# One more column for the row sum: weighted sums of an attention block in 64-column products, copied out by ScalarE

## The chip, the cores and the metric

The kernel runs on one core of a Trainium2 chip. TensorE (PE) multiplies matrices and writes PSUM, VectorE (DVE), ScalarE (ACT) and GpSimd (POOL) work on vectors, and SyncE (SP) issues the DMAs. The metric is the device time in microseconds of one execution. Three runs of the kernel before took 625.96, 629.58 and 630.68 us, a median of 629.58 us.

## The reference

One layer over 1024 real frames with 16 meta tokens in front. After an RMS norm and one input projection there are 16 attention heads of 64 value columns: 8 "fox" heads (causal, with a decay that is added to the logits) and 8 "MLA" heads (masked by chunks of 64 frames, keys and queries from low-rank latents). Each head's result is gated, and all go through one output projection, a norm and a residual. What the change touches is the softmax and its weighted sum:

```
s = einsum('bqhd,bkhd->bhqk', q[:, q0:q0 + Q_BLOCK], k[:, :kend]) * scale
s = mask_and_bias(s, q0, kend)
p = softmax(s, axis=-1)
out = einsum('bhqk,bkhd->bqhd', p, v[:, :kend])
```

The softmax is the exponential of each logit less its row's maximum, over the sum of the row.

## The kernel before, in words

The kernel has three stages. Up to about 172 us it normalizes and transposes x, and projects the latents and the values. From 172 to about 590 us it runs the 16 heads, and beside them the projections of the next heads, the gates and, late, half of the output projection. The last 39 us are the rest of the output projection and the final norm.

All large products are made in float16 with a high and a low part of each operand, as hi·hi + hi·lo + lo·hi. So the values lie in `Vt` as two blocks of 64 columns for each block of keys and head, the high part and the low part.

A head runs in four steps (`STEPS`, L701), each with two blocks of 128 rows: (7,0), (6,1), (5,2), (4,3). `run_head` calls `step` (L891) for each, so there are 64 steps. One call of `step` does, for the new pair n: the scores on PE (L800, the mask L803); the peaks of the rows on DVE (`peaks`, L810 to L815, of which `nbs` in L815 is the bias for the exponentials); the exponentials on ACT (L823). Each exponential reads the scores out of PSUM, writes `pr`, and adds up its row in `sums` by `accum_out`, which is a second instruction, ACTIVATION_READ_ACCUMULATOR. Then ACT casts the high part of the pair to float16 (`high`, L836). For the pair before, DVE makes the low part (`low`, L840) and SP issues the DMA that transposes both parts into `pT` (L919). For the pair three steps back (`LAG`) PE makes the weighted sums (`weighted`, L842), and DVE adds their two halves into `onat` (L931). The scores' PSUM buffers are free for the next pairs when the exponentials have read them: there are two of the large kind (`s2`) and one of the small kind (`s1`, blocks 0 to 2 and the end of block 7). There is one buffer `avs` for the weighted sums.

In `weighted` each block j of transposed probabilities is a stationary operand. Its high part meets the high and the low values at once, 128 columns (L849), and its low part meets the high values, 64 columns (L848). One step has 11 products of the first kind and 9 of the second, and every product has its own weight load. After a head's last step `head_end` takes the reciprocals of the row sums and GpSimd scales the head's result (L857); in the last head `tiles_end` does this for each step on DVE.

The order of the instructions on each engine is not written out: a scheduler of the framework orders each engine's queue by its own estimate of when things are ready. Each engine works its queue in order.

Of the kernel before, what the change touches and what calls it, by code (L numbers as in the profile page):

```python
# [28 lines left out]
H = 8  # L29
# [19 lines left out]
def hybrid_kernel(ctx, tc, x, meta, norm_pre, norm_post, w_in, b_f, q_norm, w_uq, kv_norm, w_ukv, w_out,  # L49
# [380 lines left out]
    def latents_V(t):  # L430
        lh, ll = lts.pop(t)
        pv = psa("pv")
        T.matmul(pv, lh, wv_h.rearrange("p h d -> p (h d)"), start=True, stop=False)
        T.matmul(pv, lh, wv_l.rearrange("p h d -> p (h d)"), start=False, stop=False)
        T.matmul(pv, ll, wv_h.rearrange("p h d -> p (h d)"), start=False, stop=True)
        vm = xs.tile([P, H, 2, HD], F16, name="vm", tag="vm", bufs=1)
        split_v(pv, scale_mu, vm[:, :, 0, :], vm[:, :, 1, :])
        SY.dma_start(vm_d[:, :, t].rearrange("h p k d -> p h k d"), vm)

    def values_out(t, ps):  # L440
        split_v(ps, scale_fu, Vt[:, t, 1 : H + 1, 0, :], Vt[:, t, 1 : H + 1, 1, :])

    def values(t):
        ps = psa("ps2")
# [373 lines left out]
    def exponentials(i, parts, nb, inv, pr, sums):  # L818

        c0 = 0  # L820
        for part, c in zip(parts, (i, NT)):
# [20 lines left out]
    def weighted(av, i, hi, lo, vh):  # L842

        n = i + 1
        avf = av.rearrange("p t d -> p (t d)")
        for j in range(n + 1):
            if j > 0:
                T.matmul(avf[:, 0:HD], lo[:, j - 1, :], Vt[:, j, vh, 0], start=False, stop=False)  # L848
            T.matmul(avf, hi[:, j, :], Vt[:, j, vh].rearrange("p t d -> p (t d)"), start=j == 0, stop=j == n)  # L849

    def head_end(onat, hh, sums):

        V.tensor_tensor(sums[:, NT - 1 : NT], sums[:, NT - 1 : NT], sums[:, NT : NT + 1], ALU.add)
        rs = at.tile([P, NT], F32, name="rs", tag="rs", bufs=2)
        V.reciprocal(rs, sums[:, 0:NT])
        o = onat[:, :, hh * HD : (hh + 1) * HD]
        G.tensor_tensor(o, o, rs.unsqueeze(2).to_broadcast([P, NT, HD]), ALU.mult)  # L857

    extras = {}
    gates = {}  # L860
# [26 lines left out]
            fn()  # L887

    steps = {}

    def step(first):  # L891

        now[0] += 1
        n = now[0]
        if first is not None:
            (ia, ib), passes, mask, mask_w, inv, sums = first[0:6]
# [11 lines left out]
            steps[n] = dict(t=(ia, ib), pr=prs, prw=pr, ph=ph, phs=(ph, ph[:, B0 * P :]), los=los, rest=first[6:])  # L908
        evacuate()
        prev = steps.get(n - 1)  # L910
        if prev is not None:
            for i, p, h, l in zip(prev["t"], prev["pr"], prev["phs"], prev["los"]):
                low(i, p, h, l)
            ph, n1 = prev["ph"].rearrange("p (b k) -> p b k", k=P), prev["prw"].rearrange("p (b k) -> p b k", k=NM)
            w0 = 1 + 8 * (prev["t"][0] + 1)
            G.tensor_tensor(ph[:, 0 : B0 + 1 : B0, 96:112], n1[:, 0 : w0 + 1 : w0, :],  # L916
                            ph[:, 0 : B0 + 1 : B0, 112:128], ALU.subtract)
            prev["pT"] = at.tile([P, NBLK * P], F16, name="pT", tag="pT", bufs=3).rearrange("p (b k) -> p b k", k=P)
            SY.dma_start_transpose(prev["pT"], prev["ph"])  # L919
        if first is not None:  # L920
            for i, p, h in zip((ia, ib), prs, steps[n]["phs"]):
                high(i, p, h)
        for fn in agenda.pop(n, ()):
            fn()
        old = steps.pop(n - LAG, None)
        if old is not None:
            (ia, ib), pT = old["t"], old["pT"]
            vh, onat, hh, after = old["rest"]
            weighted(avs[:, 1], ia, pT, pT[:, B0 + ib + 2 :, :], vh)
            weighted(avs[:, 0], ib, pT[:, B0:, :], pT[:, ia + 2 :, :], vh)  # L930
            V.tensor_reduce(onat[:, ib : ia + 1 : ia - ib, hh * HD : (hh + 1) * HD], avs.rearrange("p i t d -> p i d t"),  # L931
                            AX.X, ALU.add)
            if after is not None:
                after(ia, ib)

    def run_head(head, vh, hh, passes, mask, mask_w, inv, onat, after, each=None):

        sums = at.tile([P, NT + 1], F32, name="sums", tag="sums", bufs=2)

        def end(ia, ib):  # L940
            head_end(onat, hh, sums)
            if after is not None:
                after()

        ends = [None] * (len(STEPS) - 1) + [end]
        if each is not None:
            ends = [lambda ia, ib: each(ia, ib, sums)] * len(STEPS)

        total = sum(j[1] for j in jobs if j[0] == head)
        for k, tiles in enumerate(STEPS):  # L950
            step((tiles, passes, mask, mask_w, inv, sums, vh, onat, hh, ends[k]))
# [282 lines left out]

    def load_values(h):

        SY.dma_start(Vt[:, :, h], vm_d[h])

    later(3, lambda: load_values(0))
    for h in range(H - 1):  # L1240
# [87 lines left out]


    chains = deque()  # L1330
    ended = []

    def tiles_end(ia, ib, sums):
        if ia == NT - 1:
            V.tensor_tensor(sums[:, ia : ia + 1], sums[:, ia : ia + 1], sums[:, NT : NT + 1], ALU.add)
        both = slice(ib, ia + 1, ia - ib)
        rs = at.tile([P, 2], F32, name="rs2", tag="rs2", bufs=2)
        V.reciprocal(rs, sums[:, both])
        o = onat[:, both, HD:P]
        V.tensor_tensor(o, o, rs.unsqueeze(2).to_broadcast([P, 2, HD]), ALU.mult)  # L1340
        ended.append(sums)

        def chain():
            ps = ps_1.tile([P, 512], F32, name="pso", tag="s1")
            og = at.tile([P, 512], F32, name="og", tag="og", bufs=2)
            for k, t in enumerate((ib, ia)):
                c = slice(k * P, (k + 1) * P)
                T.transpose(ps[:, c], onat[:, t, :], ident)
                V.scalar_tensor_tensor(og[:, c], ps[:, c], OUTK, gates[7, t // 4][:, t % 4 * P : (t % 4 + 1) * P],
                                       ALU.mult, ALU.mult)  # L1350
            hi, lo = (og_part(7, k).rearrange("p (t k) -> p t k", k=P)[:, both, :] for k in range(2))
            split(og[:, 0 : 2 * P].rearrange("p (t k) -> p t k", k=P), hi, lo, A, V)
        chains.append(chain)
    for h in range(H):
# [15 lines left out]
        if h == H - 1:  # L1370
# [7 lines left out]
            for z in range(2):  # L1378
                for k in range(2):
# [9 lines left out]
    gpost = fin.tile([P, D], F32, name="gpost")  # L1389
    SY.dma_start(gpost, norm_post[0:1, :].to_broadcast([P, D]))  # L1390
    rows = {}
    slots = deque([(None, "row", 1), (at, "onat", 2)] + [(at, "pr", 2)] * 2 + [(at, f"ph{k}", 1) for k in range(NPH)]
                  + [(at, "pT", 3)] * 3 + [(at, "onat", 2), (None, "row", 1)] + [(at, "pr", 2)] * 2 + [(at, f"ph{k}", 1) for k in range(NPH)])

    def row(name):
        pl, tag, bufs = slots.popleft()
        if pl is None:
            return fin.tile([P, D], F32, name=name, tag="row", bufs=1)
        w = {"onat": D, "pr": 2 * NM + 9 * P}.get(tag, NBLK * P // 2)
        return pl.tile([P, w], F32, name=name, tag=tag, bufs=bufs)[:, 0:D]  # L1400

    def load_rows(t):
# [115 lines left out]
```

## Time and profile before

| | |
|---|---|
| median of three runs | 629.58 us (625.96 to 630.68) |
| the profiled execution | 630.68 us, of which span 628.9 us |
| PE busy, DVE busy, ACT busy | 556.4 (88%), 484.3 (77%), 422.7 (67%) |
| attention, 172 to 590 us: PE, DVE, ACT | 380.1, 336.1, 293.0 of 418 us |
| granted TensorE clock, mean | 0.979 |

The profiled execution is the slowest of the three. The span runs from the first to the last instruction; the rest of its 630.68 us lies around it. A busy PE includes the tail of each product, so its matmuls overlap in the rows; what one product costs in a stream is the distance between two starts.

### The profile page before, as it was taken

What the parts mean: (1) busy time and instruction counts of PE and PEld (TensorE: products, weight loads), DVE (VectorE), ACT (ScalarE), POOL (GpSimd) and SP (SyncE); (2) the same over time, 40 slices, a digit from 0 to 9 for tenths busy, and PEclk for the clock granted to TensorE, in tenths of its full rate; (3) what the DMA queues carried; (4) which work ended last, traced back from release to release, by engine and by line L of the source; (5) the groups of instructions that cost most, each with busy time, mean ns of one, the idle gap of its engine ahead of it and who ended that gap; (6) DMA issues with size and microseconds to landing.
All of it is one profiled execution on the core that took longest, in us unless ns stands there. A gap on an engine that the chain in (4) does not pass through costs nothing.

```text
span 628.9 us, 11509 instructions
## 1 busy us (share of the span) xinstructions
PE 556.4 (88%) x4130; PEld 330.5 (53%) x4130; DVE 484.3 (77%) x1001; ACT 422.7 (67%) x852; POOL 194.6 (31%) x282
## 2 busy tenths in 40 slices
PE   2999799989798998999998986978879979988994
PEld 1445454546456565666665553655545555554542
DVE  3778876566778886878885768789988887778666
ACT  5688877546778776657677556677785785768222
POOL 2223333362324243323331322223222322320343
PEclk9999999989899999999999998999999999999998
DMA  8858777175666988696957696597986795796963
GB/s 298 207 132 224 148 197 190 33 202 140 127 175 128 206 196 137 117 210 134 175 106 175 129 210 144 111 178 132 174 181 127 129 205 119 158 223 129 299 239 133
DMA packets 269528, 105.02 MB, mean 167 GB/s; under 512 B 234832, under 2 KB 257360, under 8 KB 269472
## 3 DMA queue, kind: packets, MB, share of 16 engines
q1 hardware_dynamic: 269472, 104.30, 73.5%
q8 instruction: 32, 0.52, 0.3%
q14 instruction: 24, 0.20, 0.1%
HBM read 48.38 MB, written 13.96 MB: 99 GB/s over the span
## 4 chain that ended last, share of the span: by engine, by line
PE 30%; DVE 26%; ACT 22%; issue 9%; DMA 9%; SPq 2%; POOL 1%; ACTq 0%; DVEq 0%; POOLq 0%
ACT pr L823 9%; DVE ph L840 5%; DVE nb L810 5%; ACT ph L836 4%; DMA pT<-ph 3%; PE psg L973 3%; PE psg L974 2%; PE s L800 2%; PE psg L975 2%; DMA wr<-in_w_in 2%; DVE nb L811 2%; PE psf L1276 2%; PE psf L1274 2%; PE psf L1275 2%; DVE nbs L815 2%
## 5 line engine op out<-in xcount | busy, mean ns | idle before, releaser
L840 DVE TENSOR_TENSOR ph<-pr,ph 128x896 f16<-128x896 f32 (+7 forms) x128 | 102.8, 812 | 32.9 <-ACT ph L836 31.6
L916 POOL TENSOR_TENSOR ph<-pr,ph 128x32 f16<-128x32 f32 x64 | 46.0, 718 | 217.4 <-issue 103.0
L800 PE MATMUL s<-st,st 128*128 128x392 f16 (+7 forms) x434 | 78.0, 306 | 18.1 <-ACT pr L823 15.1
L823 ACT ACTIVATE pr<-s,nbs,fox_inv 128x144 f32<-128x144 f32 (+8 forms) x72 | 56.1, 784 | 48.7 <-DVE nbs L815 44.3
L800 PEld LDWEIGHTS <-st 128*128 128x128 f16 x560 | 51.7, 98 | 53.5 <-issue 24.5
L823 ACT ACTIVATE pr<-s,nbs,ism 128x144 f32<-128x144 f32 (+8 forms) x72 | 56.1, 785 | 34.5 <-DVE nbs L815 28.5
L836 ACT CAST ph<-pr 128x784 f16<-128x784 f32 (+6 forms) x112 | 77.6, 736 | 0.1
L849 PE MATMUL avs<-Vt,pT 128*128 128x128 f16 x704 | 68.1, 220 | 6.1 <-DMA pT<-ph 3.2
L810 DVE TENSOR_REDUCE nb<-s 128x1 f32<-128x344 f32 (+4 forms) x80 | 68.1, 858 | 5.8 <-PE s L800 2.8
L849 PEld LDWEIGHTS <-pT 128*128 128x128 f16 x704 | 58.5, 98 | 7.3 <-DMA pT<-ph 5.1
L848 PE MATMUL avs<-Vt,pT 128*128 128x64 f16 x576 | 60.3, 193 | 0.0
L848 PEld LDWEIGHTS <-pT 128*128 128x128 f16 x576 | 50.5, 98 | 3.4 <-issue 2.7
L973 PEld LDWEIGHTS <-wp 128*128 128x128 f16 x320 | 31.9, 100 | 33.5 <-DVE st L1069 7.8
L975 PEld LDWEIGHTS <-wp 128*128 128x128 f16 x320 | 32.0, 100 | 26.2 <-issue 2.5
L974 PEld LDWEIGHTS <-wp 128*128 128x128 f16 x320 | 32.0, 100 | 24.8 <-issue 4.1
L973 PE MATMUL psq<-xAh,wp 128*128 128x264 f16 x128 | 36.1, 282 | 5.1 <-DVE st L1069 3.3
L811 DVE TENSOR_REDUCE nb<-s 128x1 f32<-128x144 f32 (+1 forms) x64 | 31.9, 499 | 6.1 <-PE s L803 5.9
L975 PE MATMUL psq<-xAh,wp 128*128 128x264 f16 x128 | 36.1, 282 | 0.0
L974 PE MATMUL psq<-xAl,wp 128*128 128x264 f16 x128 | 36.1, 282 | 0.0
L150 DVE SCALAR_TENSOR_TENSOR wp<-wr,bsc,wp 128x1024 f16<-128x1024 f32 x21 | 28.2, 1343 | 1.0 <-ACT wp L149 0.9
L973 PE MATMUL psg<-xAh,wp 128*128 128x512 f16 x64 | 25.0, 391 | 2.8 <-DVE st L1069 2.8
L973 PE MATMUL psg<-xBh,wp 128*128 128x512 f16 x64 | 25.0, 390 | 0.3 <-DVE kl L1216 0.3
(371 smaller groups left out, 1500.6 us busy)
## 6 DMA issues: line engine op xcount, KB each, us to landing
wr<-in_w_in SPq DMA_DIRECT2D x20, 512.0 KB, 4.5
wr<-in_w_in SPq DMA_DIRECT2D x26, 256.0 KB, 4.2
wor<-in_w_out SPq DMA_DIRECT2D x8, 512.0 KB
xr<-in_x SPq DMA_DIRECT2D x8, 512.0 KB, 4.3
xt<-in_x SPq DMA_DIRECT2D x7, 512.0 KB, 5.1
y_d<-ys SPq DMA_DIRECT2D x12, 256.0 KB, 2.2
y<-y_d SPq DMA_DIRECT2D x6, 512.0 KB, 4.9
out<-y SPq DMA_DIRECT2D x5, 512.0 KB
```

What stands on the lines that cost most here:

```text
L800: T.matmul(o, sta[:, i * P : (i + 1) * P], mov[:, k0 : k0 + w], start=q == 0, stop=q == len(passes) - 1 and not last)
L810: V.tensor_reduce(nb[:, k : k + 1], part, AX.X, ALU.max, negate=True)
L811: V.tensor_reduce(nb[:, 1:2], parts_b[0], AX.X, ALU.max, negate=True)
L823: A.activation(pr[:, c0:c1], part, AF.Exp, bias=nb, scale=inv, accum_out=sums[:, c : c + 1])
L836: A.copy(ph[:, 112 : 112 + W], pr)
L840: V.tensor_tensor(lo, pr[:, NM:W], ph[:, P : P + W - NM], ALU.subtract)
L848: T.matmul(avf[:, 0:HD], lo[:, j - 1, :], Vt[:, j, vh, 0], start=False, stop=False)
L849: T.matmul(avf, hi[:, j, :], Vt[:, j, vh].rearrange("p t d -> p (t d)"), start=j == 0, stop=j == n)
L916: G.tensor_tensor(ph[:, 0 : B0 + 1 : B0, 96:112], n1[:, 0 : w0 + 1 : w0, :], ph[:, 0 : B0 + 1 : B0, 112:128], ALU.subtract)
L973: T.matmul(ps[:, 0:n], hi[:, c, :], xT(0, c, c0, n), start=c == 0, stop=False)
L974: T.matmul(ps[:, 0:n], hi[:, c, :], xT(1, c, c0, n), start=False, stop=False)
L975: T.matmul(ps[:, 0:n], lo[:, c, :], xT(0, c, c0, n), start=False, stop=c == NC - 1)
```

## The change

`Vt` gets two more columns for each block and head, filled once with ones, and the two halves change places: low values first, then high values, then the ones. In `weighted` each block now has three products of 64 or 65 columns that all accumulate in the same 64 columns of `avs`: high probabilities by high values and the ones (65 columns), low probabilities by high values and the ones (65 columns), and high probabilities by low values (64 columns). Column 64 of `avs` so holds the row sum. The exponentials lose their `accum_out` and `sums` is gone. In place of the reduction on DVE, ACT copies the two blocks' 65 columns from `avs` into `ona`, a tile of each head. `head_end` and `tiles_end` take the reciprocals from `ona`'s column 64 and write the scaled result to `onat`. In the last stage the first dummy square root (which loads ACT's table) stands one step earlier, the two transposes of a pair stand ahead of both gatings, and two row buffers of the last stage use a tag of an older pool.

```diff
-    Vt = V_pool.tile([P, NT + 1, H + 1, 2, HD], F16, name="Vt")
+    Vt = V_pool.tile([P, NT + 1, H + 1, 2 * HD + 2], F16, name="Vt")
+    G.memset(Vt[:, :, :, 2 * HD :], 1.0)
...
-    avs = ps_o.tile([P, 2, 2, HD], F32, name="avs")
+    avs = ps_o.tile([P, 2, HD + 1], F32, name="avs")
...
-            A.activation(pr[:, c0:c1], part, AF.Exp, bias=nb, scale=inv, accum_out=sums[:, c : c + 1])
+            A.activation(pr[:, c0:c1], part, AF.Exp, bias=nb, scale=inv)
...
     def weighted(av, i, hi, lo, vh):
 
         n = i + 1
-        avf = av.rearrange("p t d -> p (t d)")
         for j in range(n + 1):
+            vl, v1 = Vt[:, j, vh, 0:HD], Vt[:, j, vh, HD : 2 * HD + 1]
+            T.matmul(av, hi[:, j, :], v1, start=j == 0, stop=False)
             if j > 0:
-                T.matmul(avf[:, 0:HD], lo[:, j - 1, :], Vt[:, j, vh, 0], start=False, stop=False)
-            T.matmul(avf, hi[:, j, :], Vt[:, j, vh].rearrange("p t d -> p (t d)"), start=j == 0, stop=j == n)
-
-    def head_end(onat, hh, sums):
-
-        V.tensor_tensor(sums[:, NT - 1 : NT], sums[:, NT - 1 : NT], sums[:, NT : NT + 1], ALU.add)
+                T.matmul(av, lo[:, j - 1, :], v1, start=False, stop=False)
+            T.matmul(av[:, 0:HD], hi[:, j, :], vl, start=False, stop=j == n)
+
+    def head_end(onat, hh, ona):
+
         rs = at.tile([P, NT], F32, name="rs", tag="rs", bufs=2)
-        V.reciprocal(rs, sums[:, 0:NT])
-        o = onat[:, :, hh * HD : (hh + 1) * HD]
-        G.tensor_tensor(o, o, rs.unsqueeze(2).to_broadcast([P, NT, HD]), ALU.mult)
+        V.reciprocal(rs, ona[:, :, HD])
+        G.tensor_tensor(onat[:, :, hh * HD : (hh + 1) * HD], ona[:, :, 0:HD], rs.unsqueeze(2).to_broadcast([P, NT, HD]), ALU.mult)
...
-            V.tensor_reduce(onat[:, ib : ia + 1 : ia - ib, hh * HD : (hh + 1) * HD], avs.rearrange("p i t d -> p i d t"),
-                            AX.X, ALU.add)
+            A.copy(ona[:, ib : ia + 1 : ia - ib, :], avs)
...
-    slots = deque([(None, "row", 1), (at, "onat", 2)] + [(at, "pr", 2)] * 2 + [(at, f"ph{k}", 1) for k in range(NPH)]
-                  + [(at, "pT", 3)] * 3 + [(at, "onat", 2), (None, "row", 1)] + [(at, "pr", 2)] * 2 + [(at, f"ph{k}", 1) for k in range(NPH)])
+    slots = deque([(fw, "wh", 2), (at, "onat", 2)] + [(at, "pr", 2)] * 2 + [(at, f"ph{k}", 1) for k in range(NPH)]
+                  + [(at, "pT", 3)] * 3 + [(at, "onat", 2), (fw, "wh", 2)] + [(at, "pr", 2)] * 2 + [(at, f"ph{k}", 1) for k in range(NPH)])
...
     step(None)
+    A.activation(warm, last_pr[0][:, 0:1], AF.Sqrt)
     for t in order[:3]:
...
     step(None)
-    A.activation(warm, ended[0][:, 3:4], AF.Sqrt)
     chains.popleft()()
```

On PE the start of a weighted block (the first of the kernel, behind the last score) reads, before and with the change:

```order
L849 LDWEIGHTS pT
L849 MATMUL avs<-Vt,pT 128x128
L848 LDWEIGHTS pT
L848 MATMUL avs<-Vt,pT 128x64
L849 LDWEIGHTS pT
L849 MATMUL avs<-Vt,pT 128x128
```

```order
L849 LDWEIGHTS pT
L849 MATMUL avs<-Vt,pT 128x65
L852 LDWEIGHTS pT
L852 MATMUL avs<-Vt,pT 128x64
L849 LDWEIGHTS pT
L849 MATMUL avs<-Vt,pT 128x65
L851 LDWEIGHTS pT
L851 MATMUL avs<-Vt,pT 128x65
L852 LDWEIGHTS pT
L852 MATMUL avs<-Vt,pT 128x64
```

A block pair has 31 products in place of 20. On most steps the block keeps its place behind the pair's scores; in the MLA heads the scheduler cuts it at other places than before.

On DVE, in the second head's first step (blocks 7 and 0), the rows from the peaks to the low parts read, before and with the change:

```order
L810 TENSOR_REDUCE nb<-s_2214 128x1
L810 TENSOR_REDUCE nb<-s_2213 128x1
L811 TENSOR_REDUCE nb<-s_2213 128x1
L813 TENSOR_TENSOR nb<-nb 128x1
L931 TENSOR_REDUCE onat<-avs 128x2x64
L815 TENSOR_SCALAR nbs<-nb,fox_inv 128x2
L150 SCALAR_TENSOR_TENSOR wp<-wr,bsc,wp 128x1024
```

```order
L812 TENSOR_REDUCE nb<-s_2226 128x1
L812 TENSOR_REDUCE nb<-s_2225 128x1
L813 TENSOR_REDUCE nb<-s_2225 128x1
L815 TENSOR_TENSOR nb<-nb 128x1
L152 SCALAR_TENSOR_TENSOR wp<-wr,bsc,wp 128x1024
L817 TENSOR_SCALAR nbs<-nb,fox_inv 128x2
L836 CAST ph_1705<-pr 128x144
```

The reduction is gone, and the scheduler has put the split of a weight block (L152) ahead of `nbs`.

On ACT, the same and the next step with the change (`ona` is the copy's target, `s` the scores):

```order
L933 COPY ona<-avs 128x2x65
L1131 ACTIVATE junkw,wo_sq<-wor,inv_g 128x512
L825 ACTIVATE pr<-s_2225,nbs,fox_inv 128x144
L825 ACTIVATE pr<-s_2226,nbs,fox_inv 128x696
L825 ACTIVATE pr<-s_2225,nbs,fox_inv 128x344
L1131 ACTIVATE junkw,wo_sq<-wor,inv_g 128x512
L838 CAST ph_1705<-pr 128x1040
L1063 ACTIVATE st_1696<-psq,fox_c 64x512
L1064 ACTIVATE st_1697<-psq,fox_c 64x512
L1131 ACTIVATE junkw,wo_sq<-wor,inv_g 128x512 x2
L933 COPY ona<-avs 128x2x65
L825 ACTIVATE pr<-s_2334,nbs,fox_inv 128x272
```

The copy of a step stands ahead of the same step's exponentials, in most steps directly.

## Rows read from the trace of the kernel before

**Rows 1.** Windows, attention stage: length, busy us of PE, PEld, DVE, ACT, POOL; clock, DMA.
```profile
172.00:590.00 418.00, 380.06 (x3182) 236.73 (x3181) 336.10 (x637) 292.96 (x582) 116.35 (x141) 0.98 0.78 160
```

**Rows 2.** Waits on PE, 172 to 590 us: us in total, times, longest.
```profile
PE s L800 <- ACT pr L823: 17.2, 15, 2.6
PE avs L849 <- DMA pT<-ph: 3.2, 3, 2.3
PE avs L849 <- DVE onatm L931: 3.0, 5, 1.2
...
PE psg L973 <- DVE kl L1216: 0.3, 1, 0.3
```

**Rows 3.** Chain that ended last: shares of the span by line; pieces of L931 (start, us).
```profile
ACT pr L823 9%; DVE ph L840 5%; DVE nb L810 5%; ACT ph L836 4%; DMA pT<-ph 3%; PE psg L973 3%; PE psg L974 2%; PE s L800 2%; PE psg L975 2%; DMA wr<-in_w_in 2%; DVE nb L811 2%; PE psf L1276 2%; PE psf L1274 2%; PE psf L1275 2%; DVE nbs L815 2%
...
191.57 0.07 DVE onat L931
...
540.64 0.33 DVE onatm L931
```

**Rows 4.** PE's timeline, one weighted block: start, duration, matmul.
```profile
302.83 0.22 PE L849 MATMUL avs<-Vt,pT 128*128 128x128 f16 x1
302.89 0.19 PE L848 MATMUL avs<-Vt,pT 128*128 128x64 f16 x1
302.92 0.22 PE L849 MATMUL avs<-Vt,pT 128*128 128x128 f16 x1
...
303.71 0.38 PE L973 MATMUL psq<-xBh,wp 128*128 128x512 f16 x1
```

**Rows 5.** PE's timeline: four one-column products, each with a weight load.
```profile
53.05 0.24 PE L367 MATMUL pinv<-ident,scale_f 128*128 128x1 bf16 x4
53.15 0.38 PE L304 MATMUL ps<-w2h,xAh 128*128 128x512 f16 x1
```

**Rows 6.** Groups by line: count, busy us, mean ns, idle before and what ended it.
```profile
L849 PEld LDWEIGHTS <-pT 128*128 128x128 f16 x704 | 58.5, 98 | 7.3 <-DMA pT<-ph 5.1
L931 DVE TENSOR_REDUCE onat<-avs 128x128 f32<-128x256 f32 x32 | 13.4, 418 | 0.2
L931 DVE TENSOR_REDUCE onatm<-avs 128x128 f32<-128x256 f32 x32 | 13.3, 416 | 1.7 <-PE avs L849 1.5
L823 ACT ACTIVATE pr<-s,nbs,fox_inv 128x144 f32<-128x144 f32 (+8 forms) x72 | 56.1, 784 | 48.7 <-DVE nbs L815 44.3
```

**Rows 7.** Groups by form on ACT.
```profile
L823 ACT ACTIVATION_READ_ACCUMULATOR pr<-s,nbs,fox_inv 128x1 f32 x72 | 14.0, 194 | 0.0
...
L1063 ACT ACTIVATE st<-psq,fox_c 64x264 f16<-64x264 f32 x16 | 7.6, 478 | 0.4
L1063 ACT ACTIVATE st<-psq,fox_c 64x512 f16<-64x512 f32 x8 | 5.5, 684 | 0.2
L823 ACT ACTIVATE pr<-s,nbs,fox_inv 128x272 f32<-128x272 f32 x8 | 4.6, 578 | 14.4 <-DVE nbs L815 14.3
```

**Rows 8.** Timelines of DVE and ACT in that step; in brackets idle before, releaser.
```profile
304.72 0.42 DVE L931 TENSOR_REDUCE onat<-avs 128x128 f32<-128x256 f32 x1
305.06 0.22 DVE L815 TENSOR_SCALAR nbs<-nb,fox_inv 128x2 f32<-128x2 f32 x1
305.39 0.47 ACT L823 ACTIVATE pr<-s,nbs,fox_inv 128x144 f32<-128x144 f32 x1 [0.98 <-DVE nbs L815]
305.77 0.19 ACT L823 ACTIVATION_READ_ACCUMULATOR pr<-s,nbs,fox_inv 128x1 f32 x1
305.86 0.92 ACT L823 ACTIVATE pr<-s,nbs,fox_inv 128x696 f32<-128x696 f32 x1
```

**Rows 9.** Waits on ACT, 172 to 590 us.
```profile
ACT pr L823 <- DVE nbs L815: 69.2, 43, 3.6
```

**Rows 10.** Windows: PE's last idle stretch before a slow one; that slow one.
```profile
513.80:516.00 2.20, 0.03 (x2) 0.02 (x1) 2.15 (x4) 2.14 (x6) 1.26 (x1) 1.00 0.43 128
517.10:520.30 3.20, 3.20 (x9) 1.07 (x8) 2.76 (x5) 1.70 (x3) 0.64 (x2) 0.50 0.65 122
```

**Rows 11.** DMA issues: count, KB each, median us from issue to landing.
```profile
xr<-in_x SPq DMA_DIRECT2D x8, 512.0 KB, 4.3
```

More of the change, by code (lines that the diff above doesn't have):

```diff
@@ L816, in peaks, with exponentials @@
         return nbs[:, 0:1], nbs[:, 1:2]
-    def exponentials(i, parts, nb, inv, pr, sums):
+    def exponentials(parts, nb, inv, pr):
         c0 = 0
-        for part, c in zip(parts, (i, NT)):
+        for part in parts:
             c1 = c0 + part.shape[-1]
-            A.activation(pr[:, c0:c1], part, AF.Exp, bias=nb, scale=inv, accum_out=sums[:, c : c + 1])
+            A.activation(pr[:, c0:c1], part, AF.Exp, bias=nb, scale=inv)
             c0 = c1
@@ L889, in hybrid_kernel @@
     steps = {}
+    last_pr = [None]
     def step(first):
@@ L895, in step @@
         if first is not None:
-            (ia, ib), passes, mask, mask_w, inv, sums = first[0:6]
+            (ia, ib), passes, mask, mask_w, inv = first[0:5]
             s1 = ps_1.tile([P, 512], F32, name="s1", tag="s1") if ib < 3 else None
@@ L900, in step @@
             wa, wb = NM + P * (ia + 1), NM + P * (ib + 1)
-            pr = at.tile([P, wa + wb], F32, name="pr", tag="pr", bufs=2)
+            pr = last_pr[0] = at.tile([P, wa + wb], F32, name="pr", tag="pr", bufs=2)
             prs = pr[:, 0:wa], pr[:, wa : wa + wb]
-            for i, x, nb, p in reversed(list(zip((ia, ib), sc, nbs, prs))):
-                exponentials(i, x, nb, inv, p, sums)
+            for x, nb, p in reversed(list(zip(sc, nbs, prs))):
+                exponentials(x, nb, inv, p)
             ph = phs[n % NPH]
@@ L907, in step @@
             los = ph[:, la : la + (ia + 1) * P], ph[:, lb : lb + (ib + 1) * P]
-            steps[n] = dict(t=(ia, ib), pr=prs, prw=pr, ph=ph, phs=(ph, ph[:, B0 * P :]), los=los, rest=first[6:])
+            steps[n] = dict(t=(ia, ib), pr=prs, prw=pr, ph=ph, phs=(ph, ph[:, B0 * P :]), los=los, rest=first[5:])
         evacuate()
@@ L927, in step @@
             (ia, ib), pT = old["t"], old["pT"]
-            vh, onat, hh, after = old["rest"]
+            vh, ona, after = old["rest"]
             weighted(avs[:, 1], ia, pT, pT[:, B0 + ib + 2 :, :], vh)
             weighted(avs[:, 0], ib, pT[:, B0:, :], pT[:, ia + 2 :, :], vh)
-            V.tensor_reduce(onat[:, ib : ia + 1 : ia - ib, hh * HD : (hh + 1) * HD], avs.rearrange("p i t d -> p i d t"),
-                            AX.X, ALU.add)
+            A.copy(ona[:, ib : ia + 1 : ia - ib, :], avs)
             if after is not None:
@@ L936, in run_head @@
     def run_head(head, vh, hh, passes, mask, mask_w, inv, onat, after, each=None):
-        sums = at.tile([P, NT + 1], F32, name="sums", tag="sums", bufs=2)
+        ona = at.tile([P, NT, HD + 1], F32, name="ona", tag="ona", bufs=2)
         def end(ia, ib):
-            head_end(onat, hh, sums)
+            head_end(onat, hh, ona)
             if after is not None:
@@ L946, in run_head @@
         if each is not None:
-            ends = [lambda ia, ib: each(ia, ib, sums)] * len(STEPS)
+            ends = [lambda ia, ib: each(ia, ib, ona)] * len(STEPS)
         total = sum(j[1] for j in jobs if j[0] == head)
         for k, tiles in enumerate(STEPS):
-            step((tiles, passes, mask, mask_w, inv, sums, vh, onat, hh, ends[k]))
+            step((tiles, passes, mask, mask_w, inv, vh, ona, ends[k]))
             work(head, 0.6 * total / len(STEPS))
@@ L1330, in hybrid_kernel, with tiles_end @@
     chains = deque()
[L1331 to L1335, printed above, removed]
+    def tiles_end(ia, ib, ona):
         both = slice(ib, ia + 1, ia - ib)
         rs = at.tile([P, 2], F32, name="rs2", tag="rs2", bufs=2)
[L1338 to L1341, printed above, removed]
+        V.reciprocal(rs, ona[:, both, HD])
+        V.tensor_tensor(onat[:, both, HD:P], ona[:, both, 0:HD], rs.unsqueeze(2).to_broadcast([P, 2, HD]), ALU.mult)
         def chain():
@@ L1346, in chain @@
             for k, t in enumerate((ib, ia)):
+                T.transpose(ps[:, k * P : (k + 1) * P], onat[:, t, :], ident)
+            for k, t in enumerate((ib, ia)):
                 c = slice(k * P, (k + 1) * P)
-                T.transpose(ps[:, c], onat[:, t, :], ident)
                 V.scalar_tensor_tensor(og[:, c], ps[:, c], OUTK, gates[7, t // 4][:, t % 4 * P : (t % 4 + 1) * P],
@@ L1391, in hybrid_kernel @@
     rows = {}
-    slots = deque([(None, "row", 1), (at, "onat", 2)] + [(at, "pr", 2)] * 2 + [(at, f"ph{k}", 1) for k in range(NPH)]
-                  + [(at, "pT", 3)] * 3 + [(at, "onat", 2), (None, "row", 1)] + [(at, "pr", 2)] * 2 + [(at, f"ph{k}", 1) for k in range(NPH)])
+    slots = deque([(fw, "wh", 2), (at, "onat", 2)] + [(at, "pr", 2)] * 2 + [(at, f"ph{k}", 1) for k in range(NPH)]
+                  + [(at, "pT", 3)] * 3 + [(at, "onat", 2), (fw, "wh", 2)] + [(at, "pr", 2)] * 2 + [(at, f"ph{k}", 1) for k in range(NPH)])
     def row(name):
         pl, tag, bufs = slots.popleft()
-        if pl is None:
-            return fin.tile([P, D], F32, name=name, tag="row", bufs=1)
-        w = {"onat": D, "pr": 2 * NM + 9 * P}.get(tag, NBLK * P // 2)
+        w = {"onat": D, "wh": D, "pr": 2 * NM + 9 * P}.get(tag, NBLK * P // 2)
         return pl.tile([P, w], F32, name=name, tag=tag, bufs=bufs)[:, 0:D]
```

6 lines of the change are left out of this document (3 added, 3 removed).

## The prediction

> **What bounds the kernel now.** I read the windows by stage first. In the attention stage PE is busy 380.1 of 418 us, DVE 336.1 and ACT 293.0 [rows 1]. The reader is to see that PE has only 37.9 us of idle time there, and that whatever the change does to DVE and ACT pays only where it shortens this idle time. The view of waits tells what ends it: fifteen waits of 17.2 us on exponentials that have not yet freed a scores buffer, five of 3.0 us on the reduction of L931 that frees `avs`, three of 3.2 us on transposed probabilities, and small ones, nearly all on DVE's evacuations [rows 2]. The chain that ended last then shows how the loop runs from scores to peaks to exponentials and back: the exponentials hold 9% of the span, the largest share of any line, while the reduction of L931 stands on it in only twelve pieces, 0.07 to 0.42 us each and 3.0 us together [rows 3]. So the stage is near PE's own pace, with a loop through DVE and ACT that now and then comes late.
>
> **PE: three products in place of two.** The first thing to settle is whether 704 more products with 704 more weight loads cost time. In a weighted block a product of 128 columns is followed by the next after 0.06 us and one of 64 columns after 0.03 (302.83, 302.89, 302.92) [rows 4]; taken over all of them in the trace the distances are 56 and 28 ns. Twenty products take 302.83 to 303.71, 0.88 us. That is columns alone; the weight loads, 98 ns each in their rows [rows 6], lie beside earlier products. Could the loads become the limit at 64 columns? Four one-column products, each with its own load, start 0.10 us ahead of what follows them, 25 ns each [rows 5], so loads follow each other faster than 64 columns stream. A product of 65 columns I price at 28.5 ns, between the 28 and the 56. Before: 704 x 56 + 576 x 28 = 55.6 us. After: 1280 x 28.5 + 704 x 28 = 56.2 us. The term is **+0.6 us**; its ends are -0.1 (28 for all) and +4 (30 ns for all 1984).
>
> The Trainium skill's page "TensorE: Matmul & The Clock Gate", section "Back-to-back issue gap", speaks against this change: it states that a stream of load and matmul pairs sustains one per about 81 ns at 128 columns, because the loads take their part. By that a block would not be cheaper per product for being narrower, and 704 more would cost 704 x 81 = 57 us, an estimate from that page. The trace has 56 ns at 128 columns and 28 at 64 [rows 4], so I do not follow it, but keep it as a rival.
>
> **ACT: the row sums go, a copy comes.** An exponential with its accumulator takes 578 ns for 272 columns; a copy out of PSUM without one takes 478 for 264 and 684 for 512 [rows 7], 0.83 ns a column and 259 fixed. 272 columns without accumulator are then 485, so it costs 93 ns. The read of the accumulator has a row of its own of 194 ns, but the next exponential starts when the exponential ends (305.39 + 0.47 = 305.86) and not behind that read [rows 8]. So the 144 exponentials save 144 x 0.093 = 13.4 us, with 144 x 0.194 = 27.9 as the upper end. The 64 copies of 130 columns cost 259 + 108 = 367 ns each, 23.5 us. ACT gets 10 us more work (between 4 less and 10 more), and it has 125 us of idle time.
>
> What of it lies on the path? The chain holds 9% of 628.9 us in exponentials, 57 of the two groups' 112 us (one is shown, 56.1 [rows 6]), one half. So half of 13.4 is a gain: -6.7. The copies stand directly ahead of the step's exponentials. 43 of 64 steps there wait for `nbs`, 69.2 us, 1.6 us each [rows 9], much longer than 0.37: those copies are covered. The cover is gone if the copy itself is late, which is a rival. The other 21 steps cost 21 x 0.37 at half, +3.9. ACT together: **-2.8 us** (ends -14 and +4).
>
> **DVE: the reduction goes.** 64 reductions of 417 ns, 26.7 us [rows 6], some 8% of DVE's work in this stage, and the small additions of `sums`. The lower end of the gain is what stands on the chain, 3.0 us. For the upper end I followed DVE back from each of the 36 waits of PE to its last idle moment: in 15 a reduction stands in that run, so they can shorten by at most 15 x 0.42 = 6.3 us. I take **-5.0 us**, nearer to the upper end, since 304.72 shows the worst place: there the reduction sits between the peaks and `nbs`, so that the exponential at 305.39 waits for it [rows 8]; in 16 of 64 steps it is so. The reciprocal now waits for the copy in place of the last row sum, and GpSimd's scaling for that; nobody waits for it within a step. Cost nothing.
>
> **The clock.** Four stretches of 3.4 us in the attention stage ran at a granted clock of 0.50, the lower of the two levels; ahead of the last one PE had been idle for 2.2 us [rows 10], and so it was ahead of each. Each costs half its length, 1.7 us. If these four waits shrink, some stretches go. I take one of the four: **-1.7 us**, ends 0 and -6.8.
>
> **Moved work.** Two loads of x (512 KB, 4.3 us each [rows 11]) now stand on SP's queue in the first MLA heads and not at the end, since their buffers are of an older pool and free early. Each waits for PE's last use of that buffer, with a transposition behind it; but a gate's store in the same place waits for DVE's work on the same products, which ends later. I price it at 0, with 2 x 4.3 = 8.6 as its upper end: the cover is that transposed probabilities are used two steps after their issue (418 us over 64 steps, twice 6.5 us). The memset of the ones, the earlier square root table and the last stage's transposes lie beside PE's products: 0. The scheduler gives all queues another order; I have no price for that but the spread.
>
> **Sum.** +0.6 - 2.8 - 5.0 - 1.7 = -8.9 us on the profiled execution of 630.7 gives 621.8. That execution is 1.1 us above the median of 629.6, so against the median the sum would be 620.7. I say **621.3**, 1.3% below the median.
>
> **Rivals.**
> 1. *The relief is hidden.* DVE's idle time of 82 us takes up what the reduction leaves, the waits on exponentials are set by the scores' order, and the gain is the chain's own 3.0 us less the copies: about 628. For it: 21 of the 36 waits have no reduction in the run ahead of them. Against it: the exponentials get shorter on the chain in any case.
> 2. *More than the sum.* All 15 waits shorten in full (-6.3), all four half clock stretches go (-6.8), all copies are covered (-6.7), PE +0.6: 630.7 - 19.2 = 611.5. For it: the four slow stretches hang on waits that are only just long.
> 3. *Slower: the copy holds the exponentials.* In ACT's queue the exponentials of a step stand behind a copy that waits for PE's whole weighted block, and that waits for a transposition. Price: all 64 copies on the path, 23.5, less 13.4, with nothing gained on DVE and +0.6: +10.7, 641. It decides against the change where more than 13.4 / 0.37 = 36 of the 64 copies fall outside ACT's wait for `nbs`. For it: the three waits on transpositions (up to 2.3 us [rows 2]) now stop ACT in all 64 steps, where the reduction stopped `nbs` in 16. Against it: in the step of rows 4 and 8 the block ends at 303.71 and the exponential starts only at 305.39, so the copy has 1.7 us of room.
> 4. *The loads bind.* If each added load took its 98 ns [rows 6] from PE, 704 x 0.098 = 69 us: 700. Rows 5 speak against it. The page of the Trainium skill named above would have it nearly so.
>
> **How the numbers follow.** A measurement of this kernel tells 1% (6.3 us) from no change. Forecast 45%, with its own range of 616 to 627; rival 1 25%; rival 2 12%; rival 3 15%; rival 4 3%. Below 623.3 lie three quarters of the forecast and rival 2: 46%. Within 1% lie the rest of the forecast, rival 1 and a little of rival 3: 38%. Above 635.9: 16%. The range of 8 in 10 reaches from 610, so that it holds rival 2, whose sum has half its chance below that, to 634, which leaves out most of rival 3 and rival 4.
>
> **What would show it.** In the changed kernel's timeline a weighted block of 31 products should take 0.88 to 0.92 us; over 1.2 says that the loads bind. The exponentials' fixed part should fall by some 90 ns, and the copy take 0.37 us. Most copies should follow an idle stretch of ACT that `nbs` would have ended anyway; if the view of waits shows copies waiting for PE's weighted products for more than a few us in total, and PE waiting for exponentials as long as before, rival 3 is at work. PE's idle time in the attention stage should fall from 37.9 to about 30 us, with the five waits on `avs` gone or turned to ACT. The prediction is wrong if PE's idle time stays while DVE is 27 us less busy, or if the new order of the queues brings waits that have no row here.

## The result, and the profile after

The changed kernel takes **633.1 us** (median of 10 runs, 630.7 to 634.7) against 629.4 (10 runs): ratio 1.0052, 95% interval 1.0034 to 1.0069. It is half a per cent slower, where 621.3 was forecast, 1.3% faster. By the prediction's bound of 1% that counts as no change, but the interval leaves out 1: the kernel is slower by some 3 us. The time lies inside the range given, yet none of the gain came.

The windows of the attention stage, as [rows 1], and the two stretches at the lower granted clock, as the second of [rows 10]:

```profile
172.00:590.00 418.00, 377.74 (x3803) 236.79 (x3802) 304.58 (x550) 292.72 (x506) 115.45 (x139) 0.98 0.81 162
377.60:384.20 6.60, 4.97 (x33) 2.78 (x33) 5.14 (x8) 3.68 (x8) 2.29 (x2) 0.50 1.01 171
548.20:554.80 6.60, 5.58 (x43) 3.38 (x44) 2.66 (x7) 2.67 (x6) 1.40 (x2) 0.50 0.77 146
```

DVE is 31.5 us less busy than in [rows 1], as meant; ACT is where it was, the copies in place of the accumulators. PE's idle time in this window is 40.3 us (418 less 377.7), where it was 37.9 and should have fallen to about 30. That is the sign that the prediction named for being wrong: idle time that stays while DVE is much less busy. Two slow stretches of twice the length stand for the four of before, so in this execution the clock gave nothing back. PE's waits, as [rows 2]:

```profile
PE s L802 <- ACT pr L825: 14.3, 17, 1.9
PE avs L849 <- DMA pT<-ph: 11.1, 8, 3.1
PE psq L974 <- DVE st L1070: 4.9, 3, 3.0
PE psg L974 <- DVE st L1070: 4.7, 5, 1.8
...
PE avs L849 <- ACT ona L933: 1.2, 3, 0.5
```

The reduction's wait is gone and the one on exponentials 2.9 us shorter, but the wait on transposed probabilities grew from 3.2 to 11.1 us, and the background products wait 9.6 us for DVE's evacuations (5.5 before). The waits on ACT, as [rows 9]:

```profile
ACT pr L825 <- DVE nbs L817: 54.1, 42, 2.8
ACT ona L933 <- PE avs L852: 19.9, 19, 3.2
```

On ACT the 69.2 us of waiting for `nbs` became 54.1, and 19.9 of waiting for PE's weighted products came in, with the exponentials queued behind: the picture of rival 3. The waits on DVE, before and with the change:

```profile
DVE ph L840 <- ACT ph L836: 31.6, 41, 2.2
DVE rs L855 <- ACT pr L823: 12.8, 13, 1.7
...
DVE sums L853 <- ACT pr L823: 5.1, 8, 1.0
```

```profile
DVE ph L842 <- ACT ph L838: 52.7, 47, 2.4
DVE ph L836 <- ACT pr L825: 13.2, 11, 4.2
```

DVE's wait for ACT's casts grew by 21.1 us, two thirds of its 31.5 us of relief. The second and third line before are waits that the prediction does not mention: at the ends of the heads DVE stood 17.9 us for the exponentials whose row sums it adds and divides. With the change these are gone.

A weighted block, as [rows 4], and the groups and forms that answer to [rows 6, 7]:

```profile
302.24 0.19 PE L849 MATMUL avs<-Vt,pT 128*128 128x65 f16 x1
302.27 0.19 PE L852 MATMUL avs<-Vt,pT 128*128 128x64 f16 x1
302.30 0.19 PE L849 MATMUL avs<-Vt,pT 128*128 128x65 f16 x1
...
303.18 0.38 PE L974 MATMUL psq<-xBh,wp 128*128 128x512 f16 x1
```

```profile
L849 PEld LDWEIGHTS <-pT 128*128 128x128 f16 x704 | 62.0, 98 | 17.7 <-DMA pT<-ph 15.4 <-issue 0.5
L933 ACT COPY ona<-avs 128x130 f32<-128x130 f32 x64 | 17.1, 267 | 24.3 <-PE avs L852 23.2
...
L825 ACT ACTIVATE pr<-s,nbs,fox_inv 128x272 f32<-128x272 f32 x8 | 4.6, 578 | 11.0 <-DVE nbs L817 11.0
```

The block takes 0.94 us for 0.88, the copy 267 ns where 367 was priced. The row of a 272-column exponential still says 578 ns; what the accumulator cost stands in the distance to the next instruction, 570 ns with it and 476 without.

### The profile page after: what moved, and what is told of

Same layout as the page of the kernel before. It is cut to its first block, busy times and chain, and to the rows that moved or that the text cites. A ratio compares the mean times of both kernels' runs of the same rounds, so it can differ in the third digit from the quotient of the medians.

```text
span 631.9 us, 12745 instructions
## 1 busy us (share of the span) xinstructions
PE 558.8 (88%) x4834; PEld 334.4 (53%) x4834; DVE 456.5 (72%) x921; ACT 424.0 (67%) x772; POOL 193.5 (31%) x283
## 5 line engine op out<-in xcount | busy, mean ns | idle before, releaser
L842 DVE TENSOR_TENSOR ph<-pr,ph 128x768 f16<-128x768 f32 (+7 forms) x128 | 99.4, 784 | 53.6 <-ACT ph L838 52.7
L918 POOL TENSOR_TENSOR ph<-pr,ph 128x32 f16<-128x32 f32 x64 | 49.0, 765 | 234.2 <-ACT ph L838 121.4
L802 PE MATMUL s<-st,st 128*128 128x392 f16 (+6 forms) x434 | 77.7, 309 | 13.9 <-ACT pr L825 13.4
L849 PE MATMUL avs<-Vt,pT 128*128 128x65 f16 x704 | 69.4, 195 | 12.7 <-DMA pT<-ph 11.1
L825 ACT ACTIVATE pr<-s,nbs,fox_inv 128x144 f32<-128x144 f32 (+8 forms) x72 | 52.4, 784 | 39.5 <-DVE nbs L817 36.5
L849 PEld LDWEIGHTS <-pT 128*128 128x128 f16 x704 | 62.0, 98 | 17.7 <-DMA pT<-ph 15.4
L852 PE MATMUL avs<-Vt,pT 128*128 128x64 f16 x704 | 71.2, 194 | 0.0
L825 ACT ACTIVATE pr<-s,nbs,ism 128x144 f32<-128x144 f32 (+8 forms) x72 | 52.5, 786 | 22.9 <-DVE nbs L817 21.1
L851 PE MATMUL avs<-Vt,pT 128*128 128x65 f16 x576 | 65.1, 195 | 0.0
L852 PEld LDWEIGHTS <-pT 128*128 128x128 f16 x704 | 63.2, 99 | 1.8 <-issue 1.3
L851 PEld LDWEIGHTS <-pT 128*128 128x128 f16 x576 | 53.7, 98 | 0.7 <-issue 0.3
L974 PEld LDWEIGHTS <-wp 128*128 128x128 f16 x320 | 31.2, 98 | 35.8 <-DVE st L1070 12.3
L976 PEld LDWEIGHTS <-wp 128*128 128x128 f16 x320 | 31.3, 98 | 24.6
L975 PEld LDWEIGHTS <-wp 128*128 128x128 f16 x320 | 31.3, 98 | 23.2 <-issue 2.0
L933 ACT COPY ona<-avs 128x130 f32<-128x130 f32 x64 | 17.1, 267 | 24.3 <-PE avs L852 23.2
```

The lines of the kernel that those rows point to most:

```text
L802: T.matmul(o, sta[:, i * P : (i + 1) * P], mov[:, k0 : k0 + w], start=q == 0, stop=q == len(passes) - 1 and not last)
L825: A.activation(pr[:, c0:c1], part, AF.Exp, bias=nb, scale=inv)
L842: V.tensor_tensor(lo, pr[:, NM:W], ph[:, P : P + W - NM], ALU.subtract)
L849: T.matmul(av, hi[:, j, :], v1, start=j == 0, stop=False)
L851: T.matmul(av, lo[:, j - 1, :], v1, start=False, stop=False)
L852: T.matmul(av[:, 0:HD], hi[:, j, :], vl, start=False, stop=j == n)
```

## The experiments

Ratios are to the kernel before, timed on the same chip, with 95% intervals; 0.001 is 0.63 us.

**First set: parts, each in the order that the scheduler gave it.** The theories on record: A, the narrow products cost PE time; B, the copy on ScalarE holds the exponentials; C, the last stage or moved work.

e1: the kernel before with the products alone.

```diff
-  T.matmul(avf[:, 0:HD], lo[:, j-1, :], Vt[:, j, vh, 0], ...)
-  T.matmul(avf, hi[:, j, :], Vt[:, j, vh] (128 columns), ...)
+  T.matmul(av, hi[:, j, :], Vt[:, j, vh, 0], ...)
+  T.matmul(av, lo[:, j-1, :], Vt[:, j, vh, 0], ...)
+  T.matmul(av, hi[:, j, :], Vt[:, j, vh, 1], ...)
-  V.tensor_reduce(onat[...], avs halves)
+  V.tensor_copy(onat[...], avs)
```

> The kernel before with only the three products of 64 columns (no ones, row sums still by accum_out); DVE copies avs where it added two halves. Theory A (the narrow products cost PE time): a weighted block takes 0.93 us from first product to the next, 0.06 more than before, 64 x 0.06 = 3.7 us, and the kernel comes to 632 to 634. Theory B (the copy on ScalarE holds the exponentials): 628 to 630, as before. Theory C (the new order of the queues and the moved work of the last stage): 628 to 630.

Measured 636.9, 1.0141 [1.0102, 1.0180], above the range of every theory. The products' stream (distances between starts, idle time left out, first to last weighted product) grew from 58.1 to 61.8 us, 3.7 of the 8.9 us lost.

e2: the changed kernel, `A.copy(ona, avs)` made `V.tensor_copy(ona, avs)`.

> The changed kernel with the copy from avs on DVE and not on ScalarE. Theory A: 632 to 634, as the changed kernel. Theory B: 23 us of waiting of ScalarE's copies on PE's weighted products is gone, 622 to 629. Theory C: 631 to 634.

Measured 629.6, 1.0004 [0.9978, 1.0030]: 3.0 us less than the changed kernel by the ratios. It speaks for B, at the upper end of its range, but the order of the queues changed with it.

e3: the kernel before with the last stage's edits alone (buffers of x, transposes, square root table).

> The kernel before with only the edits of the last stage (row buffers on the older pool, earlier square root table, both transposes first). Theories A and B: 629.4, no change (within 1 us). Theory C: 631 to 633, since the last stage took 40.6 us in the changed kernel's profile and 38.9 before.

Measured 630.4, 1.0013 [0.9991, 1.0035]: no change; the last stage's edits are out.

e4: the changed kernel with wide products.

```diff
-  three products of 65, 65 and 64 columns
+  T.matmul(av[:, HD:], lo[:, j-1, :], Vt[:, j, vh, HD : 2*HD+1], ...)
+  T.matmul(av, hi[:, j, :], Vt[:, j, vh, 0 : 2*HD+1], ...)
-  A.copy(ona, avs)
+  V.tensor_reduce(ona[..., 0:HD], avs halves); V.tensor_copy(ona[..., HD], avs[..., 2*HD])
```

> The changed kernel with PE's products as before (129 and 65 columns, two for each block), the row sum still by the ones, no accum_out, and the two halves added on DVE as before. Theory A: the 3.7 us of PE are back while ScalarE keeps its 13 us less, 624 to 629. Theory B: 622 to 628, since no copy stands on ScalarE. Theory C: 631 to 634.

Measured 626.2, 0.9946 [0.9917, 0.9975]: faster than both. From e1, e2 and e4 I formed theory D: a sum, with 7 us for the accumulators. The second set tested it.

e5: the kernel before, `accum_out=sums[...]` taken away.

> The kernel before, with accum_out taken off the exponentials and nothing else: the row sums are a constant that GpSimd writes once per head, so the output is not normalised (the sums are left out). Theory D (the change is a sum of parts: accumulators -7, products +2 to +5, copy on ScalarE +3.6, VectorE's relief 0): about 623, 622 to 625, with the kernel before at 630; the time stands before the exponentials' successors, the row 'PE waits for ACT pr' falls. Rival E (the accumulators alone are worth little, and it was VectorE's shorter sum or the other order of the work that gained in the other kernels): 628 to 630.

Measured 630.3, 1.0016 [0.9989, 1.0043]. The accumulators' 13 us of ScalarE gone, and no gain: theory D fell.

e6: the kernel before, the sum of the halves cut to `V.tensor_copy(onat[..., one column], avs[..., 0:1])`.

> The kernel before, with VectorE's sum of the two halves (64 of 417 ns) cut to a copy of one column per tile (about 150 ns), so 17 us less of VectorE and no other edit but a zeroing of the output rows on GpSimd; the two halves are left out of the output. Theory D (VectorE's relief turns into waiting for ScalarE): 629 to 631, no change. Rival F (VectorE's relief is worth what the forecast's term took, 5.0 us for 28 us, so 3.1 for 17): 626 to 627.5.

Measured 631.7, 1.0045 [1.0020, 1.0069]: less work, and slower, which no price of a part explains.

e7: the changed kernel, its copy held back by `G.tensor_copy(ona[..., 0:1], ph[...])`, in two halves of one PSUM tile.

> The changed kernel, with the 64 copies kept on ScalarE but issued a step later, behind the next step's exponentials and casts, from one of two alternating buffers of the weighted sums, so that a copy no longer stands ahead of the exponentials waiting for TensorE; a one-column GpSimd copy holds it there. Theory B1 (the copy costs because it waits ahead of the exponentials: 20 us of waits): 629 to 630, the time of the kernel with the copy on VectorE. Rival B2 (it costs by its own 267 ns on ScalarE, wherever it stands): 632 to 634, no change against the changed kernel.

Measured 669.2, 1.0641 [1.0598, 1.0684]. Neither theory was tested: PE now waited for the copy in 41 steps, since the two halves did not come free separately, and the copy for GpSimd. The waits on PE and ACT:

```profile
PE avs L849 <- ACT ona L896: 44.9, 41, 2.9
```

```profile
ACT ona L896 <- POOL ona L935: 31.1, 40, 1.3
```

e8: e4 with the row laid out as low part, zero, high part, one.

```diff
+  T.matmul(av[:, HD+1:], lo[:, j-1, :], Vt[:, j, vh, HD+1:], ...)
+  T.matmul(av, hi[:, j, :], Vt[:, j, vh], ...)             # 130 columns
+  V.tensor_reduce(ona, avs halves of 65)                    # brings the row sum
```

> The row of values as low part, a zero, high part, a one: the product with the high weights 130 columns wide (its two halves are low part and zero, high part and one), that with the low weights 65, and one sum over the two halves on VectorE that brings the row sum with it; no accum_out, no copy on ScalarE. It has the products of e4 without its second VectorE operation (64 of 150 ns). Theory D (VectorE's time is worth nothing): 625 to 627, as e4. Rival F: 1.7 less, 623.5 to 625.

Measured 629.0, 0.9992 [0.9969, 1.0015]: less work than e4, and 2.9 us slower. e5, e6 and e8 have one thing in common: the scheduler ordered every queue anew.

**Third set: the same parts in the order of the kernel before.** Each kernel has a table with the place of every instruction in its engine's queue, and edges of order between neighbours. They add no wait for data. Instructions that the kernel before has not stand beside their neighbours in the program.

```diff
+    for p, q in zip(seq, seq[1:]):      # seq: one engine's instructions, old order
+        tc.add_manual_dep(q, p.name, DependencyInfo(NoSync, DATA), reason="order")
```

o1 (e5's work):

> As e5 (accum_out taken off the exponentials, row sums a constant written once, so the output is not normalised), but every engine held to the issue order of the kernel before, by edges of order without waits. Theory G (the scheduler's new order, which each edit makes anew, is worth several us by itself and hid what the parts do): the accumulators' 13 us of ScalarE show as in the forecast, 3 to 7 us less, 623 to 627. Rival H (taking the accumulators away is worth nothing, whatever the order): 629 to 631.

Measured 620.3, 0.9859 [0.9832, 0.9886]: 8.9 us less, below G's range, and H is out. The 8.9 us are not ACT's alone: DVE's 17.9 us of waits for the row sums go with the accumulators, and no run parts the two. Nor is e5 its exact pair: there GpSimd wrote the constant for each head, and DVE waited 9.2 us for GpSimd at the heads' ends; o1 writes it once.

o2 (e1's work):

> As e1 (three products of 64 columns a block and a copy on VectorE, accumulators kept), held to the issue order of the kernel before. Theory G: only the products' longer stream, 61.0 for 58.1 us, so 632 to 633.5. Rival H (the products themselves cost what e1 showed): 636 to 639.

Measured 627.5, 0.9984 [0.9963, 1.0005]: no change, 9.9 us better than e1 and better than G expected; the stream was 59.7 us.

o3 (the changed kernel's work):

> The changed kernel, held up to its last stage to the issue order of the kernel before, the copy on ScalarE ahead of its step's exponentials, where the scheduler had put it too. Theory G: the sum of the parts without the new order, accumulators -3 to -7, products +3 to +5, copy +3.6: 628 to 634, and within 1 us of the sum that o1 and o2 give. Rival H (the order does nothing): 633, as the changed kernel.

Measured 626.3, **0.9963** [0.9939, 0.9987]: the same instructions, 2.3 us faster than before and 5.6 faster than in their own order. H is out; G's own figures were too high, and the sum of o1, o2 and 3.6 for the copy would have been 6.3 us faster than before.

o4 (o3, 42 copies behind the exponentials):

> As o3, but in 42 of 64 steps the copy stands on ScalarE behind its step's exponentials instead of ahead of them; nothing else differs. Theory B1 (the copy costs because the exponentials stand behind it while it waits for TensorE): 2 to 4 us less than o3. Rival B2 (it costs by its own 267 ns): no change against o3, within 1 us.

Measured 634.7, 1.0084 [1.0055, 1.0112]: 7.6 us worse than o3, which neither theory had. PE's waits in o4:

```profile
PE avs L849 <- ACT ona L933: 12.9, 8, 2.3
PE s L802 <- ACT pr L825: 7.7, 10, 1.3
```

and in o3:

```profile
PE s L802 <- ACT pr L825: 12.2, 12, 2.2
PE avs L849 <- DMA pT<-ph: 8.6, 4, 3.7
PE psq L974 <- DVE st L1070: 2.3, 2, 2.1
```

The exponentials do come earlier in o4, 7.7 for 12.2 us. But `avs` is one buffer: the next products wait 12.9 us for the copy. Neither of these two places on ACT is free: ahead the copy holds the exponentials, behind it holds PE.

**Fourth set: is it the order by itself?**

o5 (the kernel before, in the changed kernel's order):

> The kernel before with nothing changed but the issue order: up to the last stage every engine issues as in the changed kernel; VectorE's sum of the halves, which that kernel has not, stands ahead of the step whose exponentials stood behind the copy. Theory G (the new order by itself costs the 7 us that o3 gave back): 634 to 638. Rival H (the order suits this work as well as the old one; o3 gained for another reason): 629 to 631.

Measured 658.3, 1.0475 [1.0438, 1.0512]. Right in sign, far too large: PE waited 12.5 us in 7 waits for the reduction (3.0 in 5 before), whose place I had to choose, and 22.3 for exponentials (17.2 before). It does not price the order alone.

o6 (e2's work, the copy on DVE, in the old order):

> The changed kernel with the copy on VectorE in place of ScalarE (as e2), held up to its last stage to the issue order of the kernel before. Theory G (parts add in a fixed order: accumulators -9.1 by o1, products and VectorE's copy -1.8 by o2): 617 to 620; the copy's place on ScalarE then costs o3 less this, 6 to 9. Rival J (the copy costs the 3.6 that e2 and the changed kernel differ by, and the parts do not add): 622 to 624.

Measured **622.5**, 0.9897 [0.9864, 0.9929], the fastest version here that leaves nothing out, 1.0% faster than the kernel before. G's 617 to 620 was too low and J's range holds, also its figure for the copy: o3 is 4.2 us above o6. Which waits make up the 4.2 us stays open. PE waits for exponentials nearly as long in o6 (11.4 us) as in o3 (12.2); 1.5 us lie behind the last weighted product (40.4 and 38.9 us in the two profiles), and the granted clock is higher in o6, 0.986 on the mean of its runs for 0.981.

o7 (e4's work):

> As e4 (products of 129 and 65 columns, the row sum by the column of ones, sum of the halves and a copy of the sums on VectorE, no accumulators), held up to its last stage to the issue order of the kernel before. Theory G: near o1, 619 to 623. Rival K (e4's own order was already a good one, and only narrow products gain by the old order): 625 to 627, as e4.

Measured 625.0, 0.9940 [0.9916, 0.9965]: as e4 (K). One own order of seven was as good as the old one.

o8 (e8's work):

> As e8 (one sum on VectorE brings the row sums with it, so 64 operations of 150 ns fewer than o7), held up to its last stage to the issue order of the kernel before. Theory G: as o7, within 1.5 us, and not the 2.8 us slower that e8 was than e4 in orders of their own. Rival K: 628 to 630, as e8.

Measured 623.8, 0.9929 [0.9899, 0.9958], as o7; in the same order the shorter work is no longer slower.

o9 (the kernel before, nothing left out, in e5's order, which needs hardly a choice):

> The kernel before, nothing left out, held up to its last stage to the issue order that e5 had (the same instructions but for the accumulators; only the divisions that there needed no exponentials are kept behind them). Theory G (a new order by itself costs): 634 to 640, since e5 lost 10 to the same work in the old order. Rival H: 629 to 631, and e5's loss was its own.

Measured 636.2, **1.0127** [1.0099, 1.0155]: another order alone costs 8.0 us. Rival H is out.

o10 (e6's work, in the old order):

> As e6 (VectorE's 64 sums of the halves cut to a copy of one column per tile, 17 us less of VectorE; the halves are left out of the output), held to the issue order of the kernel before. Theory D (VectorE's relief turns into waiting for ScalarE): 628 to 630, no change. Rival F (the forecast's term holds, hidden in e6 by its own order): 625 to 627.

Measured 626.1, 0.9963 [0.9935, 0.9990]: 2.3 us for 17 us less DVE, in F's range and below D's. But a second thing differs: in the trace the reciprocals `rs` stand behind the head's last copy from `avs`, not ahead of it as in the kernel before, and DVE's 12.8 us of waits there are gone. So 2.3 us is not the price of the reduction alone.

**What the edges themselves do.** No run holds the kernel before to its own order, so that the edges change nothing else is argued, not measured. Against a gain from the edges speak o9, which is slower with them, and o7, which is as e4.

**The clock in it.** The granted clock of the runs moves with the order in most pairs: on the mean 0.977 in e1 and e5, 0.982 in o2 and 0.984 in o1; 0.976 in o9 and 0.980 in the kernel before beside it. Priced as in the prediction (half of the slow time is lost), that is about 3 of the 9.9 us between e1 and o2, and between 2 and 3 of o9's 8.0, an estimate. In the changed kernel it is not so: 0.984 in its own order, 0.981 in o3.

**Where a new order loses time.** An example from one step: DVE's low part, ACT ahead of the exponentials and PE ahead of a background product, in the changed kernel (start, duration; idle before, releaser):

```profile
187.48 1.22 DVE L842 TENSOR_TENSOR ph<-pr,ph 128x1024 f16<-128x1024 f32 x1 [2.44 <-ACT ph L838]
...
190.46 0.27 ACT L933 COPY ona<-avs 128x130 f32<-128x130 f32 x1
192.14 1.58 ACT L825 ACTIVATE pr<-s,nbs,fox_inv 128x272 f32<-128x272 f32 x2 [1.41 <-DVE nbs L817]
...
195.08 0.19 PE L852 MATMUL avs<-Vt,pT 128*128 128x64 f16 x1
197.07 0.39 PE L974 MATMUL psg<-xAh,wp 128*128 128x512 f16 x1 [1.80 <-DVE st L1070]
```

and the same step of o3:

```profile
185.41 1.22 DVE L842 TENSOR_TENSOR ph<-pr,ph 128x1024 f16<-128x1024 f32 x1 [2.73 <-ACT ph L838]
...
188.39 0.72 ACT L1131 ACTIVATE junkw<-wor,inv_g 128x512 bf16<-128x512 f32 x1
189.23 0.46 ACT L1063 ACTIVATE st<-psq,fox_c 64x248 f16<-64x248 f32 x1
189.60 0.25 ACT L933 COPY ona<-avs 128x130 f32<-128x130 f32 x1
190.01 1.58 ACT L825 ACTIVATE pr<-s,nbs,fox_inv 128x272 f32<-128x272 f32 x2 [0.16 <-DVE nbs L817]
...
193.96 0.19 PE L852 MATMUL avs<-Vt,pT 128*128 128x64 f16 x1
193.99 0.44 PE L802 MATMUL s<-st,st 128*128 128x328 f16 x2
194.94 0.39 PE L974 MATMUL psg<-xAh,wp 128*128 128x512 f16 x1 [0.51 <-DVE st L1070]
```

From the start of DVE's low part to the exponentials it is 4.7 us in the changed kernel and 4.6 in o3, and to the background product 9.6 and 9.5. The old order does not get there earlier; it gets more done on the way. On ACT two more pieces of work, 1.2 us, stand ahead of the copy (L1131 and L1063), so that ACT idles 0.16 us for the bias `nbs` and not 1.41. On PE the next scores stand ahead of the product that has to wait for DVE's evacuation (L1070), so that PE idles 0.51 us and not 1.80. No instruction is changed. The loss is spread over many such places, of which this is one; PE's idle time in the stage (gaps over 0.1 us, first to last weighted product) is 39.9 us in the changed kernel and 33.6 in o3.

## Why the prediction was wrong

| step | forecast, us | in the old order, us | from |
|---|---|---|---|
| accumulators | -6.7 | -8.9 | o1 |
| copies on ACT | +3.9 | +4.2 to +6.6 | o3 over o6; the upper end adds what the copies cost o6 on DVE |
| DVE | -5.0 | -3.6 | o10: 2.3 for 17 us, here 26.7; an estimate |
| PE's products | +0.6 | +4.8 | stream 58.1 to 62.9 in o3's profile |
| clock | -1.7 | no row of its own | it is part of the rows that are differences of runs |
| new order | 0 | +5.6 | changed kernel over o3 |

**The step that failed** is the last sentence of "Moved work": "The scheduler gives all queues another order; I have no price for that but the spread", and 0 in the sum. It is worth 5.6 us here (3.7 to 7.5, from the two intervals), and it turns -2.3 into +3.3. Its like cost 8.0 on unchanged work (o9), and of seven edits timed both ways six were slower in their own order, by 4.0 to 9.9 us. The order is not the whole miss: held to the old one the change gains 2.3 us where some 8 were forecast. The other term that was clearly mis-sized is PE's products.

**PE.** The mechanism was right, the size was not: loads did not bind, but the stream grew by 4.8 us, beyond the end of +4. About 1 us of this is products that fell into stretches at the lower clock, 48 of 1984 in o3's profile and none before. 64 columns in rows of 256 bytes took 29 ns for 28 (o2: +1.6 in all); in rows of 260 bytes about a quarter of all products took 32 to 36 ns, which with the 65th column made most of the rest. The Trainium skill's page "TensorE: Matmul & The Clock Gate", section "Back-to-back issue gap", with its 81 ns for a load and matmul pair at 128 columns, does not hold here: such pairs start 56 ns apart at 128 columns before and some 30 at 64 and 65 columns after, and the 57 us estimated from that page were 4.8.

**ACT.** The saving of 93 ns an exponential was right (94). With DVE's waits at the heads' ends, which the prediction left out, it came to 8.9 us, more than the half of 13.4 that was forecast. About 3 us of the 8.9 stand in the granted clock (0.984 for 0.980 in the kernel before beside it), priced as above. The copy is a quarter cheaper than priced and costs about what was forecast, which is in part luck: the sum took 21 uncovered copies, and what the profile shows is some 20 that wait for PE (19.9 us) ahead of the exponentials. That looks like rival 3's mechanism, but it is not shown to make the 4.2 us; the price of +10.7 there took all 64 and allowed DVE nothing.

**DVE.** Followed back from the waits it was worth 5.0; o10 gives 2.3 / 17 = 0.135 us for each us taken off, so 3.6 for the reductions' 26.7, nearer to the chain's 3.0, the lower end. Since o10 also moved the reciprocals, even that may be too much.

**The clock.** In the profile the number of slow stretches halved and each doubled. Over the ten runs of the changed kernel the granted clock was 0.984 on the mean, where the kernel before had 0.979 to 0.981 beside the five sets of runs: about 2 us by the prediction's price, near its -1.7. The profile alone hides this.

Without the last row the column sums to -3.5 with the lower price of the copy and -1.1 with the upper; o3 measured -2.3 [-3.8, -0.8]. This is a weak test, since the copy's price is itself taken from o3. The same prices (-8.9 for the accumulators, the growth of the stream to 61.8, 60.0 and 60.5 us, 0.135 us for each us of DVE) give -6.3 for o6, -5.7 for o7 and -6.5 for o8; measured were -6.5, -3.8 and -4.5. So with the order held the parts add to within 2 us, and not better.

Open stays why the old order suits this work so well; no run tells. An order is fitted to the durations it was made from, and o5 shows that a bad fit can cost 30 us.

## What to carry to other kernels

Where a scheduler orders the queues, an edit is two changes: the work, and a new order, which here was worth up to 1.6% by itself, more than any part. Hold the old order to price the parts, and time unchanged work in another order to learn what a result in its own order can mean. Look at the granted clock of all runs and not of the profile alone. And let a run decide which engine takes a copy that waits for another engine: here DVE was 4.2 us better than ACT (o6, o3), though DVE is the busier of the two.

## What the runs showed of the hardware

- Taking the accumulator off leaves an exponential's own row as it is (578 ns at 272 columns) and shortens the distance to the next instruction from 570 to 476 ns.
- 130 columns copied from PSUM to SBUF on ACT take 267 ns in f32, well under the 367 that the line through scaled activations gave (478 ns at 264 columns, 684 at 512).
- With rows of 260 bytes about a quarter of the 64- and 65-column products follow each other at 32 to 36 ns instead of 28 to 30 (changed kernel, o3); with rows of 256 bytes nearly none (e1, o2). Which products are the slow ones, and why, is open; padded rows were not tried.
